# SSD scan: sum of squares by two halving adds, one multiplication for the norm, its weights in the merge's split, three buffers for x and z

## Chip, core and metric

The kernel runs on one core of one Trainium2 chip. The metric is the device time of one execution in microseconds (us); lower is better. The engines are named as in the profile: PE (TensorE), DVE (VectorE), ACT (ScalarE), POOL (GpSimd) and SP (SyncE, which issues the DMAs here).

## What is computed

One decoder block over 1024 tokens of width 1024 in float32: a mixer with two parallel branches, a Mamba-2 SSD scan and gated linear attention (GLA), merged by gates; then attention to 256 memory tokens; then a SwiGLU layer; then a last norm. The change lies at the end of the SSD branch and at the start of the merge:

```python
    y = (y_diag + y_off).reshape(Bsz, S, SSD_HEADS, P) + D_skip.astype(jnp.float32)[:, None] * x_heads
    y = y.reshape(Bsz, S, SSD_D_INNER) * jax.nn.silu(z.astype(jnp.float32))
    y = rmsnorm(y.reshape(Bsz, S, G, SSD_D_INNER // G), norm_g.reshape(G, SSD_D_INNER // G))
...
    merged = jax.nn.sigmoid(g_ssd) * (y_ssd @ w_up_ssd) + jax.nn.sigmoid(g_gla) * (y_gla @ w_up_gla)
```

There are G = 2 groups of 512 channels. The norm divides each token's 512 channels by their root mean square and then multiplies each channel by its weight from `norm_g` (`ssd_norm` in the kernel).

## The kernel before

Data lie with channels on the 128 partitions and tokens along the free dimension. Large products keep float32 accuracy by splitting each operand into a high and a low part (`split`: ACT copies to the rounded high part, DVE subtracts to get the low part) and adding three products. The projections use a seven-product block scheme (`Unit`, with the steps B11, B21, T1, B22, T2, T3, T4): each step splits its weights into `whi` and `wlo`, runs 12 matmuls of 128x512 into an `acc` bank, and evicts it into `o`. T2, T3 and B22 first form sums of weights in `sa` and `raw`.

The SSD scan runs in 16 steps, one for each of 8 chunks of 128 tokens and each of 2 groups. It is interleaved with nine projection units by `run`, at about one quarter of a scan step for each unit step, and is traced at a raised priority, so that the scheduler may place it ahead of unit work. The quarters, as the class `SSD` names them:

- `load`: x (from `xbc_d`) and silu(z) (from `sz_d`) into the tile `xz`, the scan's B and C into `bc`, and the cumulated decay into `csb`, all on SP's queue.
- `lay` and `decay`: transposes of x, then `xd`, `cbm`, `e`, `csb`, `xc`.
- `scan`: the matmuls of the step into a PSUM bank `py`, and the new state.
- `gate`: y = x * D + py in four DVE instructions (one for each 128 channels), times silu(z) on POOL, squares on ACT into `sq`, and a DVE reduction over the four channel blocks into `rd` (128x128).
- `stat`: a matmul of `rd` with ones sums over the partitions, and `rsqrt` (DVE, then a power on POOL) makes `rs`, one number for each token.
- `norm`: `spread` makes a diagonal matrix `diag` from `rs` on DVE and multiplies it with ones on PE, which gives `rs` along the free dimension in a PSUM bank. Four DVE instructions then multiply y by that and by the column of `ssd_norm`, and a DMA stores y to `ys_d`.

`stat` and `norm` of a step come after the `scan` of the next one. The tile `xz` is read for the last time by POOL in `gate`, and it has two buffers.

Later, `fetch` loads `ys_d` in eight blocks of 128x1024 and splits each into high and low parts in `hl` (ACT copy, DVE subtraction). This runs beside the last projection unit (`gg[3:]`), just ahead of `dense(0, i_ys, ...)`, the first product of the merge. `fetch` serves the GLA branch's `yg_d` too.

Two mechanisms set who does what and when. `either` picks POOL or DVE for an elementwise operation by two clocks that `Meter` keeps (a fixed cost and a cost per element for each engine, both relative to the planned time of PE). The order of each engine's queue comes from a list scheduler that simulates the program (`schedule_with_timeline_sim=True`); the hardware then runs each queue in that order. All DMAs named here stand in SP's queue.

Of the kernel before, what the change touches and what calls it, by code (L numbers as in the profile page):

```python
# [9 lines left out]
F32 = mybir.dt.float32  # L10
F32R = mybir.dt.float32r
I32 = mybir.dt.int32
AF = mybir.ActivationFunctionType
ALU = mybir.AluOpType
AX = mybir.AxisListType

P = 128
# [11 lines left out]
CH = 128  # L29
# [49 lines left out]
def block_kernel(ctx: ExitStack, tc: tile.TileContext, t: dict, out: bass.AP):  # L79
    nc = tc.nc  # L80
    now = [0.0]
    PE, ACT, SP = Tensor(nc.tensor, now), nc.scalar, nc.sync
    DVE, POOL = Meter(nc.vector, now, 0.06, 1.04e-3), Meter(nc.gpsimd, now, 0.08, 2.25e-3)
# [6 lines left out]
    def pool(name, bufs=1, space=None, stack=None):  # L90
        kw = {"reuse_waits": "tile"} if space is None else {"space": space}
        return (stack or ctx).enter_context(tc.tile_pool(name=name, bufs=bufs, **kw))
# [6 lines left out]
    def dram(name, *shape):  # L99
        return dr.tile(list(shape), F32, name=name, tag=name)  # L100
# [13 lines left out]
    ys_d = dram("ys_d", D, TOK)  # L114
# [10 lines left out]
    def bank(dt=F32):  # L125
        return ps.tile([P, 512], dt, name="bank", tag="bank", bufs=4)

    add = lambda e, o, a, b: e.tensor_tensor(o, a, b, ALU.add)
    sub = lambda e, o, a, b: e.tensor_tensor(o, a, b, ALU.subtract)
    mul = lambda e, o, a, b: e.tensor_tensor(o, a, b, ALU.mult)  # L130
# [63 lines left out]
    def col(name, i=0):  # L194
        which, at = gcol[name]
        return cols[:, which, at + i:at + i + 1]
# [18 lines left out]
    def spread(p, r, n):  # L215

        for c in range(n):
            d = diag[c % 2]
            DVE.tensor_scalar(d, ident, r[:, c:c + 1], None, ALU.mult)
            PE.matmul(p[:, c * P:(c + 1) * P], ones, d, start=True, stop=True)  # L220
# [55 lines left out]
    class Unit:  # L276
# [10 lines left out]
        def load(s):  # L287
            if s.raw is None:
                s.raw = slot(s.key, (P, 2 * s.kh, 256), name="raw")
                SP.dma_start(s.raw, s.W[s.row0:s.row0 + 256 * s.kh, s.c0:s.c0 + 256].rearrange("(k p) c -> p k c", p=P))  # L290
# [124 lines left out]
    def group(units, B, then=(), nxt=None, frm=6, products=7):  # L415


        for u in units:
            u.load()
        then = list(then)  # L420
        many = len(units)
        for n, name in enumerate((CHAIN if many > 1 else SPACED)[:products]):
            for x, u in enumerate(units):
                u.step(name, B)
                if many > 1:
                    B.upto((n + 1) * B.kh - (-(x + 1) * B.kh // many))
                if n == 6 and nxt:
                    nxt.upto((x + 1) * nxt.kh // many)
                if n >= frm and then:
                    then.pop(0).load()  # L430
                while len(posts) > lag[0]:
                    settle()
                    if n < 4:
                        break
                yield
        for u in then:
            u.load()
# [101 lines left out]
    for k in range(NB):  # L539
        p = bank()  # L540
# [317 lines left out]
    sp_ = pool("ssd", 1, stack=st3)  # L858
# [6 lines left out]
    class SSD:  # L865
# [7 lines left out]

        def load(s):
            g, tk = s.g, s.tk
            s.L = sp_.tile([P, 8, CH], F32, name="xz", tag="xz", bufs=2)
            SP.dma_start(s.L[:, 0:4], xbc_d[g * 512:(g + 1) * 512, tk].rearrange("(k p) s -> p k s", p=P))
            s.BC = sp_.tile([P, 2, CH], F32, name="bc", tag="bc", bufs=2)
            for i in range(2):
                r0 = 1024 + i * 256 + g * P  # L880
                SP.dma_start(s.BC[:, i], xbc_d[r0:r0 + P, tk])
            s.csb = sp_.tile([P, GH, CH], F32, name="csb", tag="csb", bufs=2)
            SP.dma_start(s.csb.rearrange("p h s -> p (h s)"),
                         cs_d[s.i0:s.i0 + GH, :].rearrange("h s -> (h s)").partition_broadcast(P))
            SP.dma_start(s.L[:, 4:8], sz_d[g * 512:(g + 1) * 512, tk].rearrange("(k p) s -> p k s", p=P))
# [42 lines left out]
        def gate(s):  # L928
            s.y = sp_.tile([P, 4, CH], F32, name="y", tag="y", bufs=3)
            for k in range(4):  # L930
                DVE.scalar_tensor_tensor(s.y[:, k], s.L[:, k], dcol[:, s.g * 4 + k:s.g * 4 + k + 1],
                                         s.py[:, k * P:(k + 1) * P], ALU.mult, ALU.add)
            mul(POOL, s.y, s.y, s.L[:, 4:8])
            sq = sp_.tile([P, 4, CH], F32, name="sq", tag="sq", bufs=1)
            ACT.activation(sq, s.y, AF.Square)
            s.rd = sp_.tile([P, CH], F32, name="rd", tag="rd", bufs=2)
            DVE.tensor_reduce(s.rd, sq.rearrange("p k s -> p s k"), AX.X, ALU.add)

        def stat(s):
            p = bank()  # L940
# [4 lines left out]
        def norm(s):  # L945
            p = bank()
            spread(p, s.rs, 1)
            for k in range(4):
                DVE.scalar_tensor_tensor(s.y[:, k], s.y[:, k], col("ssd_norm", s.g * 4 + k), p[:, :P],
                                         ALU.mult, ALU.mult)  # L950
            SP.dma_start(ys_d[s.g * 512:(s.g + 1) * 512, s.tk].rearrange("(k p) s -> p k s", p=P), s.y)

    def ssd_steps():
# [225 lines left out]
    def paired(keys):  # L1179

        return [(lambda k=k: slot(k, (P, 2, TOK), F32R, name="hl")) for k in keys]

    def hl(slots_, k):
        if callable(slots_[k]):
            slots_[k] = slots_[k]()
        return slots_[k]
# [24 lines left out]
    EVEN, ODD = ("op",) * 8, ("op",) * 6 + ("aux",) * 2  # L1211
    i_ys, i_yg, i_wo, i_xq, i_q, i_xo = (paired(x) for x in (EVEN, ODD, EVEN, ODD, EVEN, EVEN))

    def fetch(src, dst):

        for k in range(NB):
            x = hl(dst, k)
            raw = x[:, 1].bitcast(F32)
            SP.dma_start(raw, src[k * P:(k + 1) * P, :])
            ACT.activation(x[:, 0], raw, AF.Copy)  # L1220
            sub(DVE, x[:, 1], raw, x[:, 0])
            yield

    get_ys = fetch(ys_d, i_ys)
    for n, _ in enumerate(group(gg[3:], B)):
        if n == 0:
            left.load(1)
# [88 lines left out]

    early = presum()
    run(dense(0, i_ys, post_ys, lambda o, j: gate(gs_d, o, j)), (fetch(yg_d, i_yg), 0.5), (waiting(early, 5), 1.0))
    run(dense(1, i_yg, post_yg, lambda o, j: (gate(gg_d, o, j), quad(ysg_d, o * P, 0, j))), (early, 1.0))
    run(dense(2, i_wo, residual(h1_d, s1, "norm_xattn", put_xq), quad_of(xT_d)), (early, 1.0))  # L1320

# [106 lines left out]
    for u in range(D_FF // 256):  # L1428
# [8 lines left out]
        def upost(i, j, ap, u=u, g=gate, v=up, have=set(), did=set()):  # L1437

            o = g.q(i, j)
            mul(either(ap), o, o, ap)  # L1440
            have.add((u, i, j))

            def put(name, src):
                r0 = (CHAIN.index(name) * KP + u) * P
                SP.dma_start(act_d[r0:r0 + P, :], src)
                did.add((u, name))

            for name, need, mk in (
                    ("B11", ((0, 0),), None), ("B21", ((1, 0),), None), ("B22", ((1, 1),), None),
                    ("T1", ((0, 1), (0, 0)), lambda: (v.q(0, 1), g.q(0, 1), g.q(0, 0))),  # L1450
                    ("T2", ((1, 1), "T1"), lambda: (v.q(0, 0), g.q(1, 1), v.q(0, 1))),
                    ("T3", ((1, 1), (0, 1)), lambda: (v.q(1, 1), g.q(1, 1), g.q(0, 1))),
                    ("T4", ((1, 0), "T2"), lambda: (v.q(1, 0), g.q(1, 0), v.q(0, 0)))):
                if (u, name) in did or not all((u, x) in did if isinstance(x, str) else (u, *x) in have for x in need):
                    continue
                if mk:
                    d, x, y = mk()
                    sub(either(ap), d, x, y)
                    put(name, d)
                else:  # L1460
                    put(name, g.q(*need[0]))
# [157 lines left out]
    for x, (n, k, kn) in enumerate(todo):  # L1619
        name = CHAIN[n]  # L1620
# [58 lines left out]
```

## Time and profile before

| | us |
|---|---|
| median of 3 runs | 1998.22 |
| lowest and highest run | 1995.6, 1999.11 |
| profiled execution: span | 2000.0 |
| PE busy | 1933.5 |
| DVE busy | 1330.8 |
| ACT busy | 866.3 |
| POOL busy | 658.0 |

The span is the time from the first to the last instruction of one profiled execution; the page gives no other time for that execution. The first load of the scan goes out at 400.7 us and its last store at 657.7 us. The eight loads of `ys_d` go out from 829.1 us on, and the first matmul of the merge begins at 846.4 us. Matmuls are pipelined and overlap, so their durations add up to more than the time they take. An instruction that waits holds up everything behind it in its engine's queue. Rows of a wait view read: who waited, for whom, us in total, times, longest.

### The profile page before, as it was taken

The page shows a single profiled execution, that of the slowest core. Times are in us where ns is not written, and L with a number is a line of the kernel's source. Part 1 is how long each engine was busy: PE and PEld are TensorE (multiplying, and loading weights), DVE is VectorE, ACT ScalarE, POOL GpSimd, SP SyncE. Part 2 cuts the span into 40 slices and gives each one's busy share as a digit, 9 for nine tenths or more (in the row PEclk, how much of TensorE's full clock was granted, in tenths as well). Part 3 has the DMA queues.
Part 4 walks back from the last instruction along what each step waited for, and adds up shares of the span by engine and source line. Part 5 has one row for each costly group of instructions (what it writes and reads, how often), then busy time and mean ns, then how long its engine had stood idle before and what let it go on. Part 6 is the DMA issues. An engine that isn't in the chain of part 4 may idle for free.

```text
span 2000.0 us, 26313 instructions
## 1 busy us (share of the span) xinstructions
PE 1933.5 (97%) x9772; PEld 1619.0 (81%) x9772; DVE 1330.8 (67%) x1869; ACT 866.3 (43%) x1486; POOL 658.0 (33%) x482
## 2 busy tenths in 40 slices
PE   6899999999999999999999999999999999999998
PEld 6799677787777877888888888877888888878887
DVE  5856579979887566643553427478777777784465
ACT  7434745455553555543223226453333333354243
POOL 3521253445654121112442100155444444430002
PEclk9899999999999999999999999999999999999999
DMA  9332233365663754697674310333224223176463
GB/s 303 137 123 76 97 127 116 107 199 162 181 192 103 213 162 158 226 394 242 252 249 163 106 43 22 126 124 124 79 90 134 93 85 119 72 269 220 153 228 126
DMA packets 242019, 309.59 MB, mean 155 GB/s; under 512 B 16586, under 2 KB 164276, under 8 KB 241892
## 3 DMA queue, kind: packets, MB, share of 16 engines
q1 hardware_dynamic: 241892, 307.92, 46.1%
q8 instruction: 77, 1.26, 0.3%
q14 instruction: 50, 0.41, 0.1%
HBM read 211.07 MB, written 96.80 MB: 154 GB/s over the span
## 4 chain that ended last, share of the span: by engine, by line
PE 69%; DVE 12%; DMA 7%; ACT 5%; issue 3%; POOL 3%; SPq 0%; POOLq 0%; DVEq 0%; ACTq 0%
PE acc L51 61%; PE bank L51 7%; DVE wlo L73 3%; DVE cv L73 2%; DVE o L73 1%; PE bank L55 1%; DMA raw<-in_w_in_dram 1%; DMA h_d<-ga 1%; DMA sr<-sr_d 1%; ACT whi L224 1%; DMA csb<-cs_d 1%; POOL sa L73 1%; DMA xt<-in_x_dram 1%; DMA fr<-act_d 1%; DVE fs L73 1%
## 5 line engine op out<-in xcount | busy, mean ns | idle before, releaser
L51 PE MATMUL acc<-hl,wd 128*128 128x512 f32 x1920 | 439.2, 390 | 0.2 <-DVE hl L73 0.2
L51 PEld LDWEIGHTS acc<-hl,wd 128*128 128x128 f32 x1920 | 360.0, 188 | 75.3 <-DVE hl L73 0.6
L73 DVE TENSOR_TENSOR wlo<-raw,whi 128x512 fp32r<-128x512 f32 x264 | 243.1, 925 | 64.9 <-ACT whi L224 64.5
L224 ACT ACTIVATE whi<-raw 128x512 fp32r<-128x512 f32 x272 | 169.7, 628 | 237.0 <-PE acc L51 208.1
L73 DVE TENSOR_TENSOR o<-acc,o 128x512 f32<-128x512 f32 (+1 forms) x256 | 172.5, 675 | 105.8 <-PE acc L51 91.1
L51 PE MATMUL acc<-fs 128*128 128x512 f32 (+1 forms) x792 | 156.0, 356 | 1.8 <-ACT o L1574 1.7
L51 PEld LDWEIGHTS acc<-fs 128*128 128x128 f32 x792 | 130.6, 189 | 22.8 <-ACT o L1574 2.1
L73 POOL TENSOR_TENSOR raw<-raw,sa 128x512 f32<-128x512 f32 x48 | 65.0, 1354 | 253.8 <-DVE wlo L73 250.8
L224 ACT ACTIVATE fs<-fr 128x1024 fp32r<-128x1024 f32 (+1 forms) x84 | 80.1, 984 | 112.9 <-PE acc L51 38.6
L73 DVE TENSOR_TENSOR fs<-fr,fs 128x1024 fp32r<-128x1024 f32 (+1 forms) x84 | 99.8, 1218 | 38.5 <-ACT fs L224 38.0
L224 ACT ACTIVATE whi<-sa 128x512 fp32r<-128x512 f32 x96 | 59.9, 627 | 107.5 <-PE acc L51 107.4
L73 POOL TENSOR_TENSOR sa<-raw 128x512 f32<-128x512 f32 x47 | 75.8, 1613 | 82.0 <-DMA raw<-in_w_in_dram 44.8
L73 DVE TENSOR_TENSOR wlo<-sa,whi 128x512 fp32r<-128x512 f32 x96 | 82.8, 863 | 19.0 <-ACT whi L224 17.6
L224 ACT ACTIVATE wd<-raw 128x1024 fp32r<-128x1024 f32 x40 | 42.2, 1058 | 104.9 <-PE acc L51 104.4
L73 DVE TENSOR_TENSOR wd<-raw,wd 128x1024 fp32r<-128x1024 f32 x40 | 53.9, 1349 | 50.5 <-ACT wd L224 50.0
L73 POOL TENSOR_TENSOR raw<-raw 128x512 f32<-128x512 f32 x48 | 83.0, 1730 | 5.0 <-DVE sa L73 5.0
L51 PE MATMUL acc<-B21h,whi 128*128 128x512 f32 x192 | 76.3, 398 | 3.1 <-ACT o L353 3.1
L51 PE MATMUL acc<-T1h,whi 128*128 128x512 f32 x192 | 76.3, 397 | 2.8 <-ACT whi L224 2.8
L51 PE MATMUL acc<-B22h,wlo 128*128 128x512 f32 x192 | 77.0, 401 | 1.2 <-DVE wlo L73 1.2
L51 PE MATMUL acc<-B22h,whi 128*128 128x512 f32 x192 | 75.2, 392 | 2.6 <-DVE o L73 1.5
L51 PE MATMUL acc<-T4h,whi 128*128 128x512 f32 x192 | 75.9, 395 | 1.5 <-DVE o L73 1.5
L51 PE MATMUL acc<-T1h,wlo 128*128 128x512 f32 x192 | 76.8, 400 | 0.5 <-DVE wlo L73 0.5
(386 smaller groups left out, 4771.6 us busy)
## 6 DMA issues: line engine op xcount, KB each, us to landing
raw<-in_w_in_dram SPq DMA_DIRECT2D x26, 1024.0 KB, 6.1
raw<-in_w_ffn_in_dram SPq DMA_DIRECT2D x22, 1024.0 KB, 6.3
act_d<-o SPq DMA_DIRECT2D x77, 256.0 KB, 2.1
fr<-act_d SPq DMA_DIRECT2D x35, 512.0 KB, 6.4
pre<-in_w_ffn_out_dram SPq DMA_DIRECT2D x11, 1024.0 KB, 6.1
fr<-down_d SPq DMA_DIRECT2D x20, 512.0 KB, 3.7
down_d<-pre SPq DMA_DIRECT2D x33, 256.0 KB, 5.2
raw<-in_w_xkv_dram SPq DMA_DIRECT2D x8, 1024.0 KB
```

What stands on the lines that cost most here:

```text
L51: return s.e.matmul(o, x, y, **kw)
L55: return s.e.transpose(o, x, i)
L73: return f(*a, **kw)
L224: ACT.activation(hi, src, AF.Copy)
```

## The change

- The squares of a step are added in two halving adds on DVE (128x256, then 128x128) in place of one reduction.
- The norm multiplies all of y in one DVE instruction by the PSUM bank, read four times over, without the column weights.
- The column weights `ssd_norm` are applied in `fetch` of `ys_d` instead: the ACT copy gets a scale and the DVE subtraction becomes a multiply-and-subtract. `fetch` of `yg_d` stays as it was.
- The tile `xz` has three buffers instead of two.

```diff
-            s.L = sp_.tile([P, 8, CH], F32, name="xz", tag="xz", bufs=2)
+            s.L = sp_.tile([P, 8, CH], F32, name="xz", tag="xz", bufs=3)
...
-            DVE.tensor_reduce(s.rd, sq.rearrange("p k s -> p s k"), AX.X, ALU.add)
+            add(DVE, sq[:, 0:2], sq[:, 0:2], sq[:, 2:4])
+            add(DVE, s.rd, sq[:, 0], sq[:, 1])
...
-            for k in range(4):
-                DVE.scalar_tensor_tensor(s.y[:, k], s.y[:, k], col("ssd_norm", s.g * 4 + k), p[:, :P],
-                                         ALU.mult, ALU.mult)
+            mul(DVE, s.y, s.y, p[:, :P].unsqueeze(1).to_broadcast([P, 4, CH]))
...
-    def fetch(src, dst):
+    def fetch(src, dst, gain=None):
...
+            if gain:
+                ACT.activation(x[:, 0], raw, AF.Copy, scale=col(gain, k))
+                DVE.scalar_tensor_tensor(x[:, 1], raw, col(gain, k), x[:, 0], ALU.mult, ALU.subtract)
+            else:
+                ACT.activation(x[:, 0], raw, AF.Copy)
+                sub(DVE, x[:, 1], raw, x[:, 0])
...
-    get_ys = fetch(ys_d, i_ys)
+    get_ys = fetch(ys_d, i_ys, "ssd_norm")
```

More of the change, by code (lines that the diff above doesn't have):

```diff
@@ L1219, in fetch @@
             SP.dma_start(raw, src[k * P:(k + 1) * P, :])
-            ACT.activation(x[:, 0], raw, AF.Copy)
-            sub(DVE, x[:, 1], raw, x[:, 0])
+            if gain:
[4 more added lines that the diff above has]
+                sub(DVE, x[:, 1], raw, x[:, 0])
             yield
-    get_ys = fetch(ys_d, i_ys)
+    get_ys = fetch(ys_d, i_ys, "ssd_norm")
     for n, _ in enumerate(group(gg[3:], B)):
```

## The prediction

> **What bounds the kernel now.** I read the page first, then the stretches around the SSD scan, then the waits of TensorE in them, then VectorE instruction by instruction.
>
> ```profile
> span 2000.0 us, 26313 instructions
> PE 1933.5 (97%) x9772; PEld 1619.0 (81%) x9772; DVE 1330.8 (67%) x1869; ACT 866.3 (43%) x1486; POOL 658.0 (33%) x482
> ```
>
> TensorE is busy for all but 66.5 us. An edit that takes no matmul away can only win back idle time of TensorE, and only in the stage that it touches. The stretches (columns: stretch, length, busy time and instructions of PE, PEld, DVE, ACT, POOL, then clock, DMA share, GB/s):
>
> ```profile
> 400.00:450.00 50.00, 49.89 (x296) 40.09 (x296) 37.47 (x61) 27.71 (x60) 21.63 (x17) 1.00 0.63 199
> 450.00:500.00 50.00, 45.75 (x307) 36.91 (x306) 46.13 (x78) 28.03 (x63) 26.64 (x21) 1.00 0.51 162
> 500.00:550.00 50.00, 48.40 (x313) 39.70 (x313) 42.58 (x77) 29.08 (x64) 31.57 (x23) 1.00 0.61 181
> 550.00:600.00 50.00, 48.20 (x312) 39.54 (x309) 42.66 (x82) 25.21 (x57) 27.12 (x22) 1.00 0.65 192
> 600.00:660.00 60.00, 58.75 (x309) 47.17 (x308) 43.68 (x76) 17.84 (x33) 22.45 (x21) 1.00 0.32 103
> ```
>
> Over the scan TensorE is idle for 0.11 + 4.25 + 1.60 + 1.80 + 1.25 = 9.0 us. That is the ceiling of the gain in this stage, 0.45% of the span. In the middle, 450 to 600 us, TensorE loses 7.65 us, and there VectorE is busy for 131.4 of 150 us, far above its mean of 67%. What TensorE waits for in that middle (total us, times, longest):
>
> ```profile
> PE bank L51 <- DVE y L73: 2.6, 3, 1.0
> PE bank L51 <- DVE diag L73: 2.6, 3, 1.6
> PE acc L51 <- ACT whi L224: 1.8, 2, 1.1
> PE bank L51 <- DVE xd L73: 0.4, 1, 0.4
> PE acc L51 <- DVE o L73: 0.2, 1, 0.2
> ```
>
> Of 7.6 us, 5.8 in eight waits end on a VectorE result. So here the late engine is VectorE, whose queue mixes the scan's work with the weight splits (wlo) and evictions (o) of the projection that should keep TensorE fed.
>
> **The change part by part.** First the two pieces of VectorE work that are replaced, by start times in VectorE's own order:
>
> ```profile
> 480.18 1.08 DVE L73 TENSOR_REDUCE rd<-sq 128x128 f32<-128x512 f32 x1
> 481.18 0.91 DVE L73 TENSOR_TENSOR wlo<-raw,whi 128x512 fp32r<-128x512 f32 x1
> 482.01 0.68 DVE L73 TENSOR_TENSOR xd<-bank,dtv 128x512 f32<-128x512 f32 x1
> 482.61 0.68 DVE L73 TENSOR_TENSOR o<-acc,o 128x512 f32<-128x512 f32 x1
> 483.21 0.67 DVE L73 TENSOR_TENSOR wlo<-raw,whi 128x512 fp32r<-128x512 f32 x1
> 483.81 1.11 DVE L73 SCALAR_TENSOR_TENSOR y<-y,cols,bank 128x128 f32<-128x128 f32 x4
> 484.84 1.21 DVE L73 TENSOR_TENSOR csb<-csb,bc 128x1024 f32<-128x1024 f32 x1
> ```
>
> Neighbours overlap by about 0.08 us, so I count from start to start. *The norm*: four instructions take 484.84 - 483.81 = 1.03 us. One 128x512 multiplication with one operand in PSUM is what xd is, and xd takes 482.61 - 482.01 = 0.60 us. Saved: 0.43 us a step. No row has a PSUM operand that is read four times over, so the bounds are 0.60 us (xd) and 1.03 us (no gain); I take xd's, which has the same shape and reads a broadcast operand too.
>
> *The sum of squares*: the reduction takes 1.00 us. In its place come an add of 128x256 and one of 128x128, the second of which needs the first's result. Nearest rows:
>
> ```profile
> L73 DVE TENSOR_TENSOR ssum<-ssum,sq x23: 411/685/1784, 1270.7 to 1987.8; 128x512 f32<-128x512 f32 x18, 128x256 f32<-128x256 f32 x5
> L73 DVE TENSOR_TENSOR cbm<-bank,triu 128x128 f32<-128x128 f32 x16 | 4.4, 276 | 1.8 <-PE bank L55 1.8
> L73 DVE TENSOR_TENSOR sa<-raw x1: 691/691/691, 626.3 to 626.3; 128x512 f32<-128x512 f32 x1
> L73 DVE TENSOR_TENSOR sa<-sa,raw x1: 1811/1811/1811, 627.1 to 627.1; 128x512 f32<-128x512 f32 x1
> L73 DVE TENSOR_REDUCE rd<-sq x16: 1056/1075/1099, 430.8 to 642.0; 128x128 f32<-128x512 f32 x16
> L73 DVE TENSOR_TENSOR e<-e,cbm x16: 1224/1816/2269, 413.6 to 610.5; 128x1024 f32<-128x1024 f32 x16
> ```
>
> The undisturbed price is 0.41 (the shortest ssum, a 128x256 form) + 0.28 (cbm) + about 0.1 for the dependence (the second sa starts 0.8 us after the first, which lasts 0.69) - 0.08 = 0.71 us, so 0.29 saved. But rows whose two inputs both lie in SBUF are unsteady: the same shape of sa goes from 691 to 1811 ns, e from 1224 to 2269 with a median of 1816, while the reduction, with one input, stays within 1056 to 1099. The new adds are of the unsteady kind, and the instructions behind them (wlo, xd, o) wait as long as they do. By e's median each add is 0.59 us longer, the other end is no stretch. I take 0.1 us each, nearer to none: the adds are a third or a sixth of e's length and so meet less of what disturbs it. That leaves 0.09 us, and 0.52 us a step for both edits, 8.3 us of VectorE over 16 steps.
>
> The Trainium skill, "Advanced Engine Details and Errata", section "Mode Summary", notes that VectorE's second SBUF port is shared with GpSimd, so that GpSimd and the VectorE instructions using both ports block each other. The trace has the pattern, 691 against 1811 ns. By that rule both new adds are exposed where the reduction was not, and the time would be the first rival's, 2002 us, in place of the forecast's 1993.
>
> The planner that shares out operations between VectorE and GpSimd charges 0.33 us more for the sum and 0.18 less for the norm (its constants in the code). Worked through with them, the closest of its choices in this stage stays 0.7 us from turning, so I take the same split between the engines.
>
> What of the 0.52 us reaches TensorE? Each of the eight waits of the middle has at least one step's old work ahead of it in VectorE's queue; shortened by 0.52 each, they give 8 x 0.52 = 4.2 us (bounds: 0, if GpSimd's result is later anyway, and 5.8). Outside the middle TensorE idles 1.36 us, of which I take 0.4.
>
> *Third buffer of x and z*: it lets the loads of xz start without waiting for the gate's multiplication two steps back. On SP's queue (its waits, then two of its issues in order of time):
>
> ```profile
> SPq L877 <- POOL y L73: 51.0, 14, 7.4
> ...
> 499.98 0.88 SPq L881 DMA_DIRECT2D bc<-xbc_d  x2
> 502.35 0.37 SPq L877 DMA_DIRECT2D xz<-xbc_d  x1
> ```
>
> and in the chain of work that ended last (start, length, what):
>
> ```profile
> 503.33 8.10 DMA raw<-in_w_in_dram
> 511.49 1.69 POOL sa L73
> ...
> 519.01 0.52 POOL rs L73
> 519.55 0.30 DVE diag L73
> 519.89 0.49 PE bank L51 x2
> ```
>
> SP stands 51 us in front of these loads, but that alone costs nothing: x is needed a step later. It costs where something urgent is queued behind. The chain shows one such place: the weight load at 503.33 goes out right behind the xz loads, lands 8.1 us later, and GpSimd's sums, rs and diag follow until TensorE starts late at 519.89, its longest wait (1.6 us). The loads of bc before those had gone out by 499.98 + 0.88 = 500.86, so without the pause of 1.5 us the weights come that much sooner; I expect them 1.5 us sooner and nearly all of that wait gone; 0.52 of it is counted above, so 1.1 us more. The other weight loads of the stage stand behind stores of o, which wait for evictions and not for xz; nothing is taken for them. Bounds: 0 to 1.1 us, or a loss where an earlier xz load delays a csb load on the same queue.
>
> *Weights in the split*: the eight copies and eight subtractions that bring ys in get a column factor.
>
> ```profile
> L1308 ACT ACTIVATE hl<-ga,cols x16: 707/723/727, 1029.5 to 1112.1; 128x512 fp32r<-128x512 f32 x16
> L224 ACT ACTIVATE hl<-gates x6: 615/633/635, 964.2 to 1022.1; 128x512 fp32r<-128x512 f32 x6
> L73 DVE SCALAR_TENSOR_TENSOR cv<-o,cols,cv x36: 1272/1279/2000, 286.4 to 395.6; 128x1021 f32<-128x1021 f32 x12, 128x1022 f32<-128x1022 f32 x12, 128x1023 f32<-128x1023 f32 x12
> L73 DVE TENSOR_TENSOR hl<-hl x16: 1210/1218/2151, 834.0 to 918.9; 128x1024 fp32r<-128x1024 f32 x16
> 848.71 4.62 DVE L73 TENSOR_TENSOR hl<-hl 128x1024 fp32r<-128x1024 f32 x4
> 846.37 15.80 PE L51 MATMUL acc<-hl,wd 128*128 128x512 f32 x69
> ```
>
> ScalarE pays 723 - 633 = 0.09 us each, 0.7 in all; VectorE 1279 - 1218 = 0.06 each, 0.5 in all. Most is hidden: ys is split beside the last projection unit. The last four splits, 848.71 to 853.33, fall into the first products of the merge, which run without a gap from 846.37. Four times 0.06 = 0.25 us may come through there; without any cover it would be 1.2 us. I charge 0.25.
>
> Sum against the profiled execution: 2000.0 - 4.2 - 0.4 - 1.1 + 0.25 = 1994.6 us. The page gives no time beside its span, which is 1.8 us above the median of the three runs, 1998.22 us; the same 5.4 us off that median are 1992.8 us. With the ends of the terms (4.2 down to 2, the 1.1 down to 0, the cover gone; up to 5.8) this case reaches from 1990 to 1997.
>
> **The rivals.** *Stretched adds (slower).* Place: the two adds on VectorE while GpSimd is in a two-input operation, which it is in the middle for 85.3 of 150 us. At e's median a step's two adds cost 0.71 + 2 x 0.59 = 1.89 us against 1.00, so a step is 0.89 - 0.43 = 0.46 us longer on VectorE; the eight waits grow by 3.7 us, with the fetch 1998.2 + 3.7 + 0.25 = 2002 us. It decides from a stretch of 0.36 us an add on ((0.29 + 0.43) / 2). For it: sa's 1811 ns. Against it: the short adds meet less, and the adds follow the gate's GpSimd work.
>
> *Nothing changes.* The diag waits end on GpSimd's rs, the y waits on TensorE's own order, and VectorE's freed time only lets the scan run ahead; stores keep SP's queue as late as the xz loads did. TensorE's 9.0 us stay: 1998 us. For it: diag in the chain above starts as soon as rs is done. Against it: VectorE had no pause between 480.18 and 484.84.
>
> *All of it.* The middle stops waiting for VectorE and the weights come earlier throughout: 9.0 us, 1989 us. Against it: two waits are on ScalarE's whi.
>
> *Another order (slower).* The queues are ordered by a scheduler that simulates the program, and shorter VectorE operations let it put the scan's products earlier in TensorE's queue. If diag is then waited for in each of the 16 steps instead of three in the middle, at the 0.87 us of the rows (2.6 in 3), 13 new waits cost 11.3 us, less the 5.4: 2004 us. Nothing in the trace decides this.
>
> **How the numbers follow.** A measurement of this kernel can tell about 0.2% (4.0 us) from no change. Chances: forecast 0.40 (0.33 of it faster by more than that, 0.07 within), all of it 0.12, nothing changes 0.18, stretched adds 0.17, another order 0.13. So faster 0.45, same 0.25, slower 0.30. Predicted is the likeliest, 1992.8 us. The range, 1988 to 2004 us, takes in all cases at their prices and leaves out what goes beyond them on either side. The forecast's own range is 1990 to 1997.
>
> **What would show it.** Right: the middle of the scan with VectorE busy some 6 us less in 150 and TensorE idle under 4 us; y from one instruction near 0.68 us; the adds near 0.41 and 0.28; SP's waits for xz nearly gone; ys splits of 1.28 us with no new wait of TensorE at 846 to 855. Wrong: adds with medians above 0.8 and 0.65 us; TensorE's waits for diag grown in number; weight loads still behind a blocked SP queue; or a change of TensorE's idle time in a stage the diff does not touch, which would point to the order of the queues.

## Result and the profile after

The changed kernel takes 1992.38 us (median of 20 runs) against 1998.16 us before: a ratio of 0.9971, 95% interval [0.9963, 0.9979], 5.8 us less. The profiled execution spans 1990.4 us. The stretches of the scan in it (stretch, length, then busy time of PE, PEld, DVE, ACT, POOL):

```profile
400.00:450.00 50.00, 50.00 (x299) 40.61 (x298) 34.93 (x60) 31.02 (x71) 25.59 (x19) 1.00 0.63 201
450.00:500.00 50.00, 46.97 (x311) 37.12 (x310) 44.68 (x74) 25.69 (x55) 25.94 (x21) 1.00 0.60 179
500.00:550.00 50.00, 49.64 (x331) 40.88 (x330) 42.88 (x77) 28.64 (x64) 29.74 (x24) 1.00 0.59 182
550.00:600.00 50.00, 49.44 (x327) 40.17 (x325) 43.94 (x70) 29.29 (x64) 29.52 (x23) 1.00 0.55 167
600.00:660.00 60.00, 59.33 (x292) 48.25 (x289) 41.84 (x73) 17.91 (x30) 20.07 (x18) 1.00 0.46 140
```

TensorE is idle for 0 + 3.03 + 0.36 + 0.56 + 0.67 = 4.6 us in place of 9.0 (6.3 us in a second profile of the same kernel). VectorE is as busy in the middle as before (131.5 of 150 us), but TensorE gets through more there, 969 matmul records in place of 932: the time freed on VectorE was filled with other work of its queue. Who TensorE waits for between 450 and 600 us:

```profile
PE bank L51 <- DVE diag L73: 1.5, 4, 0.6
PE bank L51 <- DVE y L73: 1.1, 1, 1.1
PE acc L51 <- DVE wlo L73: 0.9, 2, 0.5
PE acc L51 <- DVE o L73: 0.2, 1, 0.2
PE acc L51 <- ACT whi L224: 0.2, 1, 0.2
```

The waits for y and diag, 5.2 us before, are 2.6 now. The wait for ScalarE's whi fell as well, from 1.8 to 0.2 us (0.9 in the second profile), which the prediction had not counted on. The changed instructions of the scan (minimum, median, maximum in ns):

```profile
L73 DVE TENSOR_TENSOR y<-y,bank x16: 670/675/687, 440.5 to 648.5; 128x512 f32<-128x512 f32 x16
L73 DVE TENSOR_TENSOR sq<-sq x16: 407/414/1046, 428.0 to 635.9; 128x256 f32<-128x256 f32 x16
L73 DVE TENSOR_TENSOR rd<-sq x16: 275/292/1020, 428.5 to 636.3; 128x128 f32<-128x128 f32 x16
```

the adds' means in the scan (shape, count, then busy us and mean ns):

```profile
L73 DVE TENSOR_TENSOR sq<-sq 128x256 f32<-128x256 f32 x16 | 7.9, 493 | 0.0
L73 DVE TENSOR_TENSOR rd<-sq 128x128 f32<-128x128 f32 x16 | 5.3, 333 | 0.3
```

and one pair of adds in VectorE's order:

```profile
428.02 0.42 DVE L73 TENSOR_TENSOR sq<-sq 128x256 f32<-128x256 f32 x1
428.48 0.29 DVE L73 TENSOR_TENSOR rd<-sq 128x128 f32<-128x128 f32 x1
428.69 1.12 DVE L73 SCALAR_TENSOR_TENSOR y<-xz,dcol,bank 128x128 f32<-128x128 f32 x4
```

The splits of ys, and in the timeline the first products of the merge:

```profile
L1220 ACT ACTIVATE hl<-hl,cols x8: 1152/1154/1159, 823.7 to 841.5; 128x1024 fp32r<-128x1024 f32 x8
L73 DVE SCALAR_TENSOR_TENSOR hl<-hl,cols x8: 1277/1282/1286, 824.9 to 843.3; 128x1024 fp32r<-128x1024 f32 x8
```

```profile
837.50 18.75 PE L51 MATMUL acc<-hl,wd 128*128 128x512 f32 x82
```

TensorE goes through the merge's start without a gap: the dearer splits are hidden. SP still stands before the loads of xz:

```profile
SPq L877 <- POOL y L73: 45.6, 13, 6.9
```

A warning on reading two profiles: their spans differ by 9.6 us, the medians by 5.8. Part of that lies ahead of anything that the diff touches, in the first 100 us. Before, then after:

```profile
0.00:100.00 100.00, 75.72 (x561) 71.68 (x562) 73.98 (x95) 60.36 (x118) 45.73 (x40) 0.91 0.64 220
```

```profile
0.00:100.00 100.00, 79.08 (x590) 75.04 (x591) 73.77 (x99) 60.86 (x118) 45.92 (x40) 0.93 0.65 223
```

TensorE is busy there for 3.4 us more, and other profiles of this study give up to 82.7, whatever the kernel. From the first xz load to the first matmul of the merge the trace before has 846.4 - 400.7 = 445.7 us, the one after 837.5 - 398.9 = 438.6, and a second one of the changed kernel 836.8 - 396.6 = 440.2: 5.5 to 7.1 us less, and profiles of one kernel differ by 1.6 us. A profile also shows one execution, which need not be a typical one. In the other runs the time of the profiled execution is 1.7 to 1.8 us longer than its span, so by estimate the one before took 2001.7 us, 3.5 above the median of its kernel, and its 9.0 us of idle TensorE may be more than usual. The profiled execution of `norm` (below) took 1998.18 us where the median of its kernel is 1993.42, and that of `no_norm` 1994.36 where the median is 1998.68. By their profiles alone these two kernels would change places. So the times below decide what a part is worth, and a profile tells only who waits for whom.

### The profile page after: what moved, and what is told of

Same layout as the page of the kernel before. It is cut to its first block, busy times and chain, and to the rows that moved or that the text cites. A ratio compares the mean times of both kernels' runs of the same rounds, so it can differ in the third digit from the quotient of the medians.

```text
span 1990.4 us, 26272 instructions
## 1 busy us (share of the span) xinstructions
PE 1933.6 (97%) x9772; PEld 1619.8 (81%) x9772; DVE 1315.8 (66%) x1837; ACT 867.6 (44%) x1486; POOL 659.7 (33%) x482
## 4 chain that ended last, share of the span: by engine, by line
PE 71%; DVE 11%; ACT 5%; DMA 5%; issue 4%; POOL 3%; SPq 1%; POOLq 0%; DVEq 0%; ACTq 0%
PE acc L51 63%; PE bank L51 8%; DVE wlo L73 2%; DVE cv L73 2%; DMA raw<-in_w_in_dram 1%; DVE o L73 1%; PE bank L55 1%; ACT whi L224 1%; DMA xt<-in_x_dram 1%; DMA sr<-sr_d 1%; DVE fs L73 1%; DMA fr<-act_d 1%; POOL raw L73 1%; POOL sa L73 1%; DMA yg_d<-qk 1%
## 5 line engine op out<-in xcount | busy, mean ns | idle before, releaser
L51 PE MATMUL acc<-hl,wd 128*128 128x512 f32 x1920 | 438.6, 389 | 0.0
L51 PE MATMUL acc<-B11h,whi 128*128 128x512 f32 x192 | 75.6, 394 | 2.3 <-ACT whi L224 2.3
L73 POOL TENSOR_TENSOR o<-o 128x512 f32<-128x512 f32 x29 | 49.2, 1702 | 83.4 <-DVE o L73 72.1
```

Source lines behind the costliest of these rows:

```text
L51: return s.e.matmul(o, x, y, **kw)
L73: return f(*a, **kw)
```

## Experiments: each part alone

Three kernels make one part of the change in the kernel before; a fourth adds work to VectorE. All were timed beside the kernel before on the same chip, and the ratio is to that.

The adds alone (`adds`):

```diff
-            DVE.tensor_reduce(s.rd, sq.rearrange("p k s -> p s k"), AX.X, ALU.add)
+            add(DVE, sq[:, 0:2], sq[:, 0:2], sq[:, 2:4])
+            add(DVE, s.rd, sq[:, 0], sq[:, 1])
```

> Only the two halving adds, in the kernel before. Theory A (the middle of the scan is bound by VectorE's queue, and what counts is VectorE time taken out of it): the adds take 0.71 us from start to start in place of 1.00, with 0.1 us of stretch each about 0.2 us a step; 38% or less of the whole change's VectorE saving, so 1 to 2.3 us faster, ratio 0.9988 to 0.9995. Theory B (the third buffer brought the gain): no change, ratio 1.000. Theory C (the gain is luck of the new order of the queues and does not follow VectorE's time): any sign, and the parts do not add up to the whole.

Measured: 1.0004 [0.9995, 1.0012]. No gain that shows, where theory A expected 1 to 2.3 us.

The norm and its weights alone (`norm`):

```diff
-            for k in range(4):
-                DVE.scalar_tensor_tensor(s.y[:, k], s.y[:, k], col("ssd_norm", s.g * 4 + k), p[:, :P],
-                                         ALU.mult, ALU.mult)
+            mul(DVE, s.y, s.y, p[:, :P].unsqueeze(1).to_broadcast([P, 4, CH]))
...
+                ACT.activation(x[:, 0], raw, AF.Copy, scale=col(gain, k))
+                DVE.scalar_tensor_tensor(x[:, 1], raw, col(gain, k), x[:, 0], ALU.mult, ALU.subtract)
...
```

> Only the norm in one multiplication, with the weights in the split of the merge, in the kernel before. Theory A: 0.43 us a step less on VectorE, the larger part of the saving: 3 to 4 us faster, ratio 0.9980 to 0.9985, and no new wait of TensorE at the first products of the merge. Theory B: no change. Theory C: any sign, not adding up with the other parts.

Measured: 0.9983 [0.9974, 0.9992], 3.4 us faster, as theory A has it, and the first products of the merge run without a gap in its trace too.

The third buffer alone (`xz3`):

```diff
-            s.L = sp_.tile([P, 8, CH], F32, name="xz", tag="xz", bufs=2)
+            s.L = sp_.tile([P, 8, CH], F32, name="xz", tag="xz", bufs=3)
```

> Only the third buffer of x and z, in the kernel before. Theory A: SP stood before these loads for 45.6 us in the whole change as against 51.0, so hardly anything is moved: within 1 us, ratio 0.9995 to 1.0005. Theory B: most of the gain, 4 to 6 us, ratio about 0.9975. Theory C: any sign.

Measured: 1.0002 [0.9993, 1.0011], as theory A has it. Theory B, that the buffer brought the gain, falls.

More work on VectorE (`load`):

```diff
+            junk = sp_.tile([P, 4, CH], F32, name="junk", tag="junk", bufs=1)
+            mul(DVE, junk, s.y, p[:, :P].unsqueeze(1).to_broadcast([P, 4, CH]))
```

> The kernel before with one more VectorE multiplication a step that nobody reads (128x512, one operand in PSUM, 0.60 us from start to start), 9.6 us of VectorE in all. Theory A: slower by about as much as 0.6 us of VectorE is worth in the change, so 5 to 8 us, ratio 1.0025 to 1.004, with TensorE idle between 450 and 600 us up by as much. If VectorE is not the bound there (GpSimd or latency is): within 2 us.

Measured: 1.0015 [1.0006, 1.0023], 3.0 us slower. The sign is theory A's, the size is not: 9.6 us of VectorE cost 3.0, a third. In its profile TensorE's waits for the four multiplications are replaced by waits for the added one:

```profile
PE bank L51 <- DVE junk L73: 4.4, 5, 1.7
```

while the idle time of the stage hardly differs (9.4 us), so the forecast rise of it is not seen. The profiled execution was the fastest of this kernel (1998.35 us, median 2000.77), and does not show the 3.0 us of the medians.

## Experiments: each part undone

The parts alone came to 2.2 us, the whole to 5.8. So each part was also undone in the changed kernel, which completes all eight combinations of the three parts. These runs were made on another chip than the parts alone, again with the kernel before beside them. The diffs are those above, reversed. `no_adds`:

> The changed kernel with the reduction back in place of the two adds. The whole change measured 0.9971 and its parts alone 1.0004 (adds), 0.9983 (norm) and 1.0002 (third buffer), 0.9989 together: 3.6 us are missing. Theory A (VectorE time counts, the parts alone differ only by noise): 0.998, 1 to 2 us given back. Theory D (the parts help each other: the third buffer or the adds pay once the norm has relieved VectorE): 0.998 to 0.9985 if the adds belong to it, 0.997 if they don't. Theory C (new order of the queues each time): any value between 0.996 and 1.001.

Measured: 0.9973 [0.9962, 0.9984]. Nothing that shows is given back, where theory A expected 1 to 2 us. `no_norm`:

> The changed kernel with the four multiplications of the norm, and the split of ys without weights; the adds and the third buffer stay. Theory A: 0.9995, as the adds alone should have given, and most of the gain is lost. Theory D with adds and buffer helping each other without the norm: 0.998. Theory C: any value.

Measured: 0.9998 [0.9985, 1.0011]. Without the norm nothing that shows is left of the gain. `no_xz3`:

> The changed kernel with two buffers of x and z. Theory A: 0.997, nothing given back, since SP still stood 45.6 us before these loads. Theory D (the buffer pays once VectorE is relieved): 0.998 or above, 2 to 3.5 us given back. Theory C: any value.

Measured: 0.9980 [0.9969, 0.9992]. This is where theory D begins (0.998 or above), and the interval reaches theory A's 0.997 as well.

Each part now stands in four pairs of kernels that differ in it alone. The differences of their ratios:

| part | beside neither | beside one other part | beside both | mean | us |
|---|---|---|---|---|---|
| norm, weights in the split | -0.0017 | -0.0024 (adds), -0.0029 (buffer) | -0.0027 | -0.0024 | -4.8 |
| third buffer | +0.0002 | -0.0006 (adds), -0.0010 (norm) | -0.0009 | -0.0006 | -1.2 |
| two adds | +0.0004 | -0.0003 (norm), -0.0004 (buffer) | -0.0002 | -0.0001 | -0.3 |

An interval of a kernel is about 0.001 to either side; taken as independent, the mean of four differences is known to 0.001 x sqrt(8) / 4 = 0.0007, or 1.4 us. The norm is shown clearly; the buffer and the adds are not told apart from nothing. The means add up to 6.3 us, the whole is 5.8. Whether the parts help each other (theory D) is not settled: the 0.0018 (3.6 us) missing after the first four runs is about the joint error of the four ratios, 0.0017. The one hint of it is the buffer, which gives +0.0002 and -0.0006 without the norm and -0.0010 and -0.0009 beside it. Theory C does not fit: the norm has the same sign and nearly the same size in all four surroundings, each with its own order of the queues.

## Experiments: the causes by themselves

Does the gain follow VectorE's time, whatever is taken out of its queue? `diag_only` leaves the whole change out and moves the diagonal matrix to ScalarE:

```diff
-            spread(p, s.rs, 1)
+            ACT.activation(diag[0], ident, AF.Copy, scale=s.rs)
+            PE.matmul(p[:, :P], ones, diag[0], start=True, stop=True)
```

> The kernel before with one change that is not in the diff: the diagonal matrix on ScalarE, which takes 16 x 0.53 us off VectorE's queue in the scan (8.5 us), about as much as the norm's 6.9 us. If the gain follows VectorE's time in the scan, wherever it is taken out: 3 to 5 us faster like the norm (4.8 us in the mean of the four pairs that differ in it), ratio 0.9975 to 0.9985. If it was the norm's own bank or order that counted: 0.9995 or above.

Measured: 0.9973 [0.9963, 0.9983], 5.4 us faster, a little over the forecast. Before, this instruction took 8.5 us of VectorE in 16 pieces, and it held the queue besides: in the waits of VectorE before,

```profile
DVE diag L73 <- POOL rs L73: 8.9, 12, 1.8
```

all that stood behind diag stood for those 8.9 us too. In the trace of `diag_only`, its row and TensorE's waits:

```profile
L947 ACT ACTIVATE diag<-ident,rs x16: 386/390/404, 439.1 to 645.4; 128x128 f32<-128x128 f32 x16
```

```profile
PE bank L51 <- DVE y L73: 2.4, 3, 1.2
PE bank L51 <- DVE rd L73: 0.9, 1, 0.9
PE bank L51 <- ACT diag L947: 0.4, 1, 0.4
PE acc L51 <- DVE wlo L73: 0.2, 1, 0.2
```

TensorE waits for diag for 0.4 us in place of 3.3 over the scan, and for y as before. So an edit that is not in the change gains as much by taking work off VectorE's queue.

This does not yet show that VectorE's time as such is what counts. The three edits that moved the time (the norm, the added multiplication, diag) all lie in `norm`, on one chain: `rs`, diag, the product with ones into a PSUM bank, and the multiplications that hold this bank. `bank()` has four banks for all products of the scan; if they are taken in turn, in the order of the code, the bank of a step's `norm` goes next to the first product of `lay` (`bank<-bc`) of a later step. TensorE's three waits for y in the kernel before all end there, just after the norm's four multiplications, and none after the four of `gate`. The first of them:

```profile
471.47 1.11 DVE L73 SCALAR_TENSOR_TENSOR y<-y,cols,bank 128x128 f32<-128x128 f32 x4
472.64 0.49 PE L51 MATMUL bank<-bc 128*128 128x128 f32 x2 [0.90 <-DVE y L73]
```

With the waits for diag (3.3 us) that makes 5.9 of TensorE's 9.0 us on this bank. The adds work on the same queue ahead of the chain, take 3.4 us off VectorE and gained nothing that shows. So the rival that this chain holds TensorE up, and not VectorE's time wherever it is spent, fits the runs as well, and none parts the two: no kernel here takes as much as the norm's 6.9 us off VectorE outside the chain. The sums of waits do not settle it either. In the profile of `norm`, with its gain of 3.4 us, TensorE waits 2.4 us for y and 1.9 for diag; in that of `no_norm`, without gain, 1.7 and 1.7.

The same edit on top of the change (`diag_act`, and later `diag_act2` beside the changed kernel, `after2`):

> The changed kernel with the diagonal matrix of the norm made on ScalarE (copy with a column factor) in place of VectorE, whose 16 took 489 ns on average in the scan. If VectorE's time still counts: 0.45 us a step less, 7 us of VectorE, 2 to 3 us of time, ratio 0.9955 to 0.996. If ScalarE's queue, where it stands behind eight decays and exponentials of some 4 us a step, hands it out later than VectorE did: TensorE waits for diag grow and the ratio is 0.998 or above.

> The changed kernel with the diagonal matrix on ScalarE, beside the changed kernel on the same chip: 0.996 again, 2 us or more below the changed kernel, if VectorE's time still counts after the change. If the first measurement was chance: as the changed kernel, 0.997.

> The changed kernel itself, as the base of this call: 0.9971 with an interval that overlaps 0.9963 to 0.9979.

Measured: 0.9959 [0.9945, 0.9973] and 0.9962 [0.9947, 0.9977]; the changed kernel beside the second 0.9968 [0.9958, 0.9979]. Both medians, 1990.54 and 1990.29 us, lie below every median of the changed kernel (1992.38 and 1992.28), but the intervals overlap: some 1 to 2 us, likely and not settled. In the trace of `diag_act` TensorE is idle for 2.3 us of the scan (2.8 in that of `diag_act2`):

```profile
400.00:660.00 260.00, 257.70 (x1580) 213.73 (x1579) 189.59 (x336) 139.44 (x302) 129.24 (x102) 1.00 0.59 179
```

There is little idle time of TensorE left to win in this stage.

Is it SP's hold before the xz loads that the third buffer shortens? `xz_act` goes back to two buffers and issues these loads from ScalarE's queue:

```diff
-            s.L = sp_.tile([P, 8, CH], F32, name="xz", tag="xz", bufs=3)
-            SP.dma_start(s.L[:, 0:4], xbc_d[...
+            s.L = sp_.tile([P, 8, CH], F32, name="xz", tag="xz", bufs=2)
+            ACT.dma_start(s.L[:, 0:4], xbc_d[...
...
-            SP.dma_start(s.L[:, 4:8], sz_d[...
+            ACT.dma_start(s.L[:, 4:8], sz_d[...
```

> The changed kernel with two buffers of x and z and their loads issued from ScalarE's queue, so that no load or store on SP's queue stands behind an xz load. The third buffer is worth 1.2 us in the mean of four pairs, though SP went on waiting before xz loads. If it was SP's hold that it shortened: as the changed kernel or better, 0.997 or below, and weight loads up to 2 us sooner. If the hold costs nothing: 0.998, as with two buffers on SP; above that if ScalarE's issue time or its waits cost.

Measured: 0.9979 [0.9968, 0.9989], the same as two buffers on SP (0.9980). The weight loads did come sooner. In `no_xz3` and then in `xz_act` (start, time of the issue):

```profile
499.94 0.50 SPq L290 DMA_DIRECT2D raw<-in_w_in_dram  x1
528.53 0.43 SPq L290 DMA_DIRECT2D raw<-in_w_in_dram  x1
```

```profile
490.04 0.39 SPq L290 DMA_DIRECT2D raw<-in_w_in_dram  x1
519.48 0.39 SPq L290 DMA_DIRECT2D raw<-in_w_in_dram  x1
```

These are 9.9 and 9.1 us sooner, of which 2.8 is the earlier start of the scan (394.5 in place of 397.3), and no time came of it. SP's hold costs nothing here, or ScalarE's issues cost what it saves; the runs do not part these two.

## Why the prediction was right, step by step

*The total.* Forecast 5.4 us less, measured 5.8 (1992.8 and 1992.38 us). That it comes this close is partly luck: the interval of the measurement alone is 1.6 us to either side, the price of VectorE's time and the step behind the buffer's 1.1 us do not hold (below), and the wait for whi fell though nothing was counted for it.

*The bound.* Right as far as the runs go: work on VectorE's queue in the scan holds TensorE up. Three edits show it: the norm, diag moved away, and the added multiplication. That any VectorE time counts alike, as the sum had it, is not shown, since all three lie on the chain through the norm's bank. For two of TensorE's four waits for diag, 0.66 and 1.60 us, VectorE itself had stood waiting for GpSimd's `rs` (1.09 and 1.04 us), so the rival *Nothing changes* had part of these waits right.

*The norm.* Right in mechanism: one instruction of 675 ns, the xd price, and no surcharge for the operand in PSUM that is read four times. It is the larger share of the 0.52 us a step, 0.43 of it, so by the prediction's terms it was worth 0.43 / 0.52 of 4.6 us, less 0.25 for the splits: 3.6 us. It measured 4.8, and the difference is within the error of 1.4. The charge of 0.25 us was not needed; TensorE had no gap at the merge.

*The adds.* The stretch was priced at 0.1 us each and measured 0.08 (493 - 414) and 0.04 (333 - 292). The stretch exists, and where it comes it is as long as the rival had it: 1046 - 414 = 0.63 us for the first add, 1020 - 292 = 0.73 for the second, against the rival's 0.59. But it came in 3 of the 32 adds. In the trace these three, and no others, start while GpSimd runs a 128x512 operation, and they end 0.15 to 0.29 us after it:

```profile
475.78 1.28 POOL L73 TENSOR_TENSOR sa<-sa,raw 128x512 f32<-128x512 f32 x1
476.31 1.04 DVE L73 TENSOR_TENSOR sq<-sq 128x256 f32<-128x256 f32 x1
```

The other 29 start while GpSimd runs nothing. So the 0.1 us an add was right in the mean for the reason given, that the adds seldom meet GpSimd's work; where one does, it is stretched as much as a long instruction. (By undisturbed durations they are a third and nearly a quarter of e's 1.22 us, not a third and a sixth.) So the first rival did not come about. Undisturbed, the pair takes 428.69 - 428.02 = 0.67 us, forecast 0.71. With the mean stretch a step saves 1.00 - 0.67 - 0.08 - 0.04 = 0.21 us, more than the 0.09 forecast, and yet nothing shows in the time (0.3 us, with an error of 1.4).

The Trainium skill, "VectorE: DVE Perf Modes", section "Rules for kernel authors", calls the reduction the slowest of VectorE's operations and advises to consider restructuring it on a hot path. The durations of this pair agree, 1075 ns against 414 and 292; the kernel's time, on this path, did not follow.

*The price of VectorE's time.* The prediction turned 8.3 us of VectorE into 4.6 us, a rate of 0.55, by counting waits. The runs give 0.70 for the norm (4.8 of 6.9), 0.31 for the added work (3.0 of 9.6), 0.31 for diag if its hold on the queue is counted (5.4 of 17.4) and 0.64 if not, and for the adds 0.3 of 3.4, which may be zero. So the forecast's total rests on a rate that fits the norm and is too high for the added work; that theory A expected 5 to 8 us there was this error. What sets the rate is not settled. The waits and the order of the banks suggest that it is what TensorE has standing behind the instruction: a PSUM bank that the norm, or in `load` the added multiplication, sets free, and little behind rd. That is argued and not shown.

*The third buffer.* The size agrees (1.1 forecast, 1.2 measured), but 1.2 within 1.4 is not told apart from nothing, and the step behind it was wrong, so the agreement is luck. SP's waits were to vanish and are 45.6 us in place of 51.0, and the weight load of the chain that the prediction followed still goes out behind a pair of held xz loads:

```profile
497.87 1.31 POOL y L73
499.20 0.37 SPq L877
499.62 0.50 SPq L885
500.17 6.69 DMA raw<-in_w_in_dram
...
515.35 0.30 DVE diag L73
515.69 0.49 PE bank L51 x2
```

The scheduler used the free buffer to place the loads a step further ahead (the third goes out at 404.1 us, before at 427.3; the last at 577.6, before at 597.5), where each waits for a gate again, with little less in all. TensorE's longest wait for diag did fall from 1.6 to 0.7 us, but not by that road. What the buffer does, if it does anything, stays open; no run was made with more than three.

*What the profile was to show.* Right: TensorE idle under 4 us in the middle (3.95, though 5.2 in the second profile), the durations, the merge without a new wait. Wrong: VectorE 6 us less busy in the middle (131.4 before, 131.5 after), since the freed time is refilled at once in a fixed stretch of time, and SP's waits.

## What to carry to other kernels

Where a secondary engine's in-order queue feeds the bound engine, look for the instruction whose result the bound engine waits for, and for those that stand idle in the queue on a third engine's result; here shortening the one and moving the other gained 4.8 and 5.4 us, while shortening a third instruction of the same queue gained nothing that shows. Time taken off a busy engine need not be a gain. The parts of an edit of a few microseconds in 2000 are better told apart by all their combinations than by each part alone: a single ratio was known to about 0.001 here, a mean of four pairs to 0.0007. A freed buffer goes where the scheduler puts it; check in the trace that the wait it was meant to end is gone.

## What the runs showed of the hardware

Two-input VectorE operations on SBUF vary by a factor of two to four (275 to 1020 ns for 128x128), the same operation with one operand in PSUM does not (670 to 687 ns for 128x512), even where that operand is read four times over. In the trace of the changed kernel exactly those adds are stretched that start while GpSimd runs a 128x512 operation (3 of 32), and they end just after it. In `diag_act` six of the first adds start during GpSimd's 128x1 power for `rs` and keep their 0.41 to 0.42 us, so not every GpSimd instruction does it. The reduction, with one input, started twice during GpSimd's work before (549.49 and 600.82 us) and kept its length, 1.07 and 1.09 us. The Trainium skill, "SBUF — State Buffer", section "Who interferes with whom", states that a VectorE instruction with two SBUF inputs contends with a GpSimd instruction that reads SBUF; the rows agree with it, and no run here takes GpSimd away to prove it. (The Trainium skill's section "Mode Summary", which the prediction cites for this, speaks of VectorE's two-port modes and does not name two inputs.) Even diag, a one-input operation on SBUF, ran from 270 to 1410 ns on VectorE, long in 4 of 16 cases before, each of which starts during a GpSimd instruction, and steadily, 386 to 404 ns, on ScalarE.
